# A fourth buffer for loaded weights, and early weights moved behind the last forgetting head, in a two-layer hybrid decoder

## The chip, the cores and the metric

The kernel runs on one core of a Trainium2 chip. The metric is device time in microseconds (us) of one execution, lower is better. Engines are named as in the profile: PE (matrix products), DVE, ACT and POOL (elementwise work), SP (issues the loads of weights).

## The reference

Sixteen learned tokens are put ahead of 512 input tokens (T = 528). Two layers of width 1024 follow. Each normalizes, makes one combined input projection, feeds eight forgetting-attention heads (64 wide) and four retention heads (128 wide), projects their joint output, and ends with a gated feed-forward part of 22 tiles of 128 columns:

```python
proj = einsum('bld,dc->blc', rmsnorm(h, attn_norm_g), w_in)
fq, fk, fv, flog, rq, rk, rv, rg = split(proj)
# forgetting head: s = q.k/sqrt(64) + c[t] - c[s], c = cumsum(log f); softmax over s <= t; then p.v
# retention head: o_t = sum_{s<=t} gamma^(t-s) (q_t.k_s) v_s, in chunks of 128
ret_out = silu(rg) * head_groupnorm(ret, ret_gn_g)
h = h + concat([fox_out, ret_out]) @ w_out
ff = silu(hn @ w_gate) * (hn @ w_up)          # hn = rmsnorm(h, ffn_norm_g)
h = h + ff @ w_down
```

After a last norm the 16 learned tokens are dropped. All is float32.

## The kernel before, in words

Activations are kept transposed, 128 features to a tile and all tokens along it. Every float32 operand is split into a high and a low part (names ending in h and l, or hi and lo): ACT makes the high part by a rounding copy (a "cast"), DVE or POOL subtracts it from the original for the low part, and a product is three products on PE: high by high, high by low, low by high.

Weights come as *jobs*. `fetch` (L161) takes a tile of a ring named `raw`, 512 KB each with three buffers, and has SP load the weight into it. `convert` (L176) makes its high part (ACT, L202) and low part (L205; on POOL for the jobs marked so, in eight pieces of 128 columns). A buffer is free for the next load when the last subtraction has read it. A job is converted some steps ahead of its use, while the job before it is multiplied. `dense_steps` (L208) makes one step per contracted tile of 128; its products are at L228.

The order of PE's work is written out by hand: `merge` and `spread` place the steps of the heads into the steps of the projections, and PE works exactly in that order. The order on ACT, DVE, POOL and SP is set when the program is built by a scheduler that goes by its own costs and by priorities. Each engine works through its own queue strictly in order.

A layer goes through these stages. The two groups of four forgetting heads and four retention heads are worked on while the combined projection still runs. The last forgetting pair, `fox[3]`, and the retention heads 2 and 3 run beside the second round of the output projection (`out_proj(l, 1, ...)`, four jobs `op` for the pairs of output tiles m2 = 0 to 3). The weights of m2 = 2 and 3 go into tiles that earlier heads have left (`spent`: qs0, qs1, kx0, kx1 and rqh, rql, rkh, rkl). Of a forgetting head the change touches this: the probabilities are transposed on PE (L446), cast to `pth` by ACT and `ptl` by DVE (L153, L154, `turn`), and multiplied with the values at L613; ACT copies the result to `ol` at L616, DVE adds it at L617. Of a retention head: its result is squared and cast (`sqh`, L796, ACT; `sq`, `sql`, L797 and L798, DVE), summed by PE at L309 against a tile of ones, and the norm follows (L314 on ACT).

The feed-forward part makes tiles f = 0 and 1 (f < PLAIN) by plain products. From f = 2 on a *Unit* computes gate and up together from seven half-size products in three accumulators, the PSUM banks x, y and z; `keep` copies what x holds at three points of its sum (L1008), and at the third adds bank y to it on DVE (L1011). A unit has a `head`, a `middle` and a `tail` of steps, and between the middle and tail of unit f a part of the down projection of the round before is placed (`down`). Rounds of up to four tiles are multiplied with `w_down` while the next round's units run; the last round's sums stand alone at the end of the layer, eight groups of four steps in layer 0 and sixteen in layer 1, where the real tokens are taken in two parts.

Of the kernel before, what the change touches and what calls it, by code (L numbers as in the profile page):

```python
# [10 lines left out]
F32 = mybir.dt.float32  # L11
# [28 lines left out]
def hybrid_kernel(ctx, tc, x_t, w_in, w_fl, w_out, w_gate, w_up, w_down, vecs, b_fg, rope, decay, mask, ident, out_t):  # L40
# [120 lines left out]
    def fetch(j):  # L161
        job = jobs[j]
        if "load" in job:
            job["load"]()
        elif "raw" not in job:
            n = job["src"].shape[1]
            job["raw"] = wp.tile([128, NK, 128], F32, name="raw", tag="raw", bufs=3)
            if j > 1:
                nc.sync.dma_start(job["raw"], job["src"]) if n == NK else \
                    nc.sync.dma_start(job["raw"][:, 0:n], job["src"])  # L170
# [5 lines left out]
    def convert(j, upto=NK, pinned=False):  # L176

        if j >= len(jobs):
            return
        job = jobs[j]  # L180
        fetch(j)
        if "make" in job:
            if "w" not in job:
                n = job["n"]
                hi, lo = (wring(job["ring"] + p) for p in ("whi", "wlo"))
                job["w"] = [(NK, hi, lo)]
                job["make"](hi[:, 0:n], lo[:, 0:n])
            return
        n = job["src"].shape[1]
        if "w" not in job:  # L190
            job["w"] = job["own"]() if job["own"] else \
                [(NK, *[wring(i) for i in ("whi", "wlo")])]
            job["split"] = 0
        sub = nc.gpsimd.tensor_sub if job["pool"] else nc.vector.tensor_sub
        while job["split"] < min(n, upto):
            c0 = job["split"]
            c1 = min(n, c0 + (2 if j < 2 and c0 < 4 else 4))
            size, hi, lo = job["w"][c0 // job["w"][0][0]]
            o = c0 % size
            hi, lo = hi[:, o:o + c1 - c0], lo[:, o:o + c1 - c0]  # L200
            with tc.high_priority() if j == 5 else ExitStack():
                pin(nc.scalar.copy(hi, job["raw"][:, c0:c1]), pinned)  # L202
            step = 1 if job["pool"] else c1 - c0
            for c in range(0, c1 - c0, step):
                pin(sub(lo[:, c:c + step], job["raw"][:, c0 + c:c0 + c + step], hi[:, c:c + step].bitcast(F32)), pinned)  # L205
            job["split"] = c1

    def dense_steps(src, parts, pool=False, banks=False, ahead=(1, 4), own=None, wait=None, far=False):  # L208

        j = len(jobs)
        jobs.append({"src": src, "pool": pool, "own": own})
# [297 lines left out]
    def fox_steps(g, st, ly, real):  # L511
# [86 lines left out]
        def product(s):  # L598
# [14 lines left out]
                    nc.tensor.matmul(po[:, c0:SEQ], v[:, j, :], pp[:, j, META + c0:T],  # L613
                                     start=(j == 0 and i == 0), stop=(j == 4))
            with tc.high_priority():
                nc.scalar.copy(ol[a0:a1, META:T], po[b0:b1, :])  # L616
                nc.vector.tensor_add(mt[a0:a1, META:T], po[a0:a1, :], ol[a0:a1, META:T])  # L617
            if s == 1:

# [217 lines left out]
                    nc.vector.tensor_add(sv(h[m], real), pv(ps, real), sv(h[m], real))  # L837
        return go

    def out_proj(l, rnd, mix, real):  # L840

        cols = REAL if real else FULL
        xs = lambda k: mix[k]["mix"]
# [1 line left out]
        def spent(m2):  # L845
# [2 lines left out]

        return sum([dense_steps(w_out[l, rnd, m2], [(4 * s, xs, 4, cols, add_h(2 * m2 + s, real)) for s in range(2)],
                                rnd == 0 or m2 < 3, rnd == 1 and m2 == 1, () if rnd == 1 and m2 == 3 else (1, 4),  # L850
                                spent(m2) if rnd == 1 and m2 > 1 else None, far=rnd == 1 and m2 == 1) for m2 in range(NK // 2)], [])

    def ffn(l, st, real, last):
        QC = REAL if real else FULL
# [93 lines left out]
        class Unit:  # L948
# [11 lines left out]

            def load(self):
                if "a" not in self.t:
                    for n, src, pool, tag, bufs in (("a", w_gate, wp, "raw", 3), ("b", w_up, phase["ffn"], "fraw", 2)):
# [39 lines left out]
            def keep(self, i):  # L1003
                def go():
                    if i == 0:
                        self.t["e"] = fft("e", F32, (128, 3, w), 2)
                    with tc.high_priority():
                        nc.scalar.copy(self.t["e"][:, i], self.t["x"][:, 0:w])  # L1008
                        if i == 2:
                            e3 = self.t["e"][:, 2]  # L1010
                            nc.vector.tensor_add(e3, self.t["y"][:, 0:w], e3)  # L1011
                return go

            def done(self):
# [32 lines left out]
        def down_job(p, f0, f1):  # L1047
# [4 lines left out]
            def load():  # L1052
                if t:
                    return
                t["r"] = wp.tile([128, NK, 128], F32, name="raw", tag="raw", bufs=3)
# [38 lines left out]
        for r, (f0, f1) in enumerate(ROUNDS):  # L1094
            for f in range(f0, f1):
# [10 lines left out]
                u = units[f]  # L1106
                u.rest()
                steps += u.middle()
                if f == NF - 1:
                    u.last()  # L1110
                    steps += u.tail()
                p, g0, g1 = fills.pop(0)
                j = down_job(p, g0, g1)
                steps += down(j, 0, 2 * p, g0, g1, not real or f < PLAIN + 2)
                if f < NF - 1:
                    u.last()
                    steps += u.tail()
                steps += down(j, 1, 2 * p + 1, g0, g1, f == PLAIN)
            fills = [(p, f0, f1) for p in range(NK // 2)]
        n = f1 - f0  # L1120
        js = [down_job(p, f0, f1) for p, _, _ in fills]
        if not last:
            for p in range(NK // 2):
                for s in range(2):
                    steps += down(js[p], s, 2 * p + s, f0, f1, False)
        else:


# [13 lines left out]
            for c0, c1 in (PA, PB):  # L1142
                for m in range(NK):
                    ps = []

                    def bank(ps=ps):
                        if not ps:
                            ps.append(psum_a())
                        return ps[0]

                    rnd += product(js[m // 2], m % 2 * n, lambda k, c0=c0, c1=c1: [t[:, c0:c1] for t in acts[f0 + k]],
                                   bank, True, True, n, add_part(m, c0, c1, bank))
# [129 lines left out]
    def layer(l):  # L1282
# [194 lines left out]
```

## Time and profile before

| what | value |
|---|---|
| median of three runs | 1274.67 us (1273.5 to 1275.17) |
| profiled execution | 1274.18 us |
| its span in the trace | 1272.4 us |
| PE busy | 1253.2 us, 98% of the span |
| mean granted clock of PE | 0.992 |
| DVE, ACT, POOL busy | 991.0, 709.1, 296.0 us |

The span is what the trace covers; the profiled execution's own time is 1.8 us longer. A wait in the profile is idle time of an engine, put down to whatever came last. The granted clock is a share of PE's full speed, so 0.50 means that matmuls take twice as long.

### The profile page before, as it was taken

Reading aid. Unit: us, or ns where it says so; the run is one execution under the profiler, and the core shown is the slowest. Engines: PE = TensorE matmul, PEld = TensorE weight load, DVE = VectorE, ACT = ScalarE, POOL = GpSimd, SP = SyncE. Lnnn points to the kernel's source line nnn. Section 1 sums busy time; section 2 is a strip of 40 time slices with the busy share of each in tenths; the row PEclk is TensorE's granted clock in tenths of the full one; section 3 lists DMA queues with packets and bytes.
Section 4 is the critical chain, followed back from the end, with each engine's and each line's share of the span. In section 5 each row is a group of like instructions: output and inputs, shape, how many; then the busy total and the mean of one; then the engine's idle time right before and its main releaser. Section 6 shows DMA issues by size and latency. Waiting matters only on the chain.

```text
span 1272.4 us, 23678 instructions
## 1 busy us (share of the span) xinstructions
PE 1253.2 (98%) x9291; PEld 1199.6 (94%) x9291; DVE 991.0 (78%) x1797; ACT 709.1 (56%) x1313; POOL 296.0 (23%) x584
## 2 busy tenths in 40 slices
PE   9999999899999999999999999998999999999997
PEld 9999999899999999999999988997789999999997
DVE  7887756789987777777776876467899878888875
ACT  7767656676444444444466665566765444444444
POOL 4545655520000000000035555555200000000000
PEclk9999999999999999999999999998999999999999
DMA  6222222221333333332312222222313333333321
GB/s 217 67 76 75 68 69 91 67 100 60 111 113 100 100 100 100 100 100 67 117 60 83 76 75 79 72 76 83 112 59 130 99 100 100 100 101 108 108 67 67
DMA packets 43343, 116.21 MB, mean 91 GB/s; under 512 B 5088, under 2 KB 9952, under 8 KB 43232
## 3 DMA queue, kind: packets, MB, share of 16 engines
q1 hardware_dynamic: 42800, 114.41, 28.1%
q8 instruction: 73, 1.20, 0.4%
q10 hardware_dynamic: 432, 0.29, 0.1%
q14 instruction: 38, 0.31, 0.1%
HBM read 112.58 MB, written 2.10 MB: 90 GB/s over the span
## 4 chain that ended last, share of the span: by engine, by line
PE 94%; DVE 3%; ACT 1%; POOL 1%; DMA 1%; issue 0%; DVEq 0%; ACTq 0%
PE psd L228 28%; PE psa L941 20%; PE psd L941 14%; PE psd L1077 13%; PE psa L228 5%; PE psa L1077 5%; PE psa L613 2%; PE psa L446 2%; PE psa L543 1%; PE psa L783 1%; PE psa L747 1%; POOL wlo L205 1%; PE psa L407 1%; DMA raw<-w_out 1%; PE psa L309 0%
## 5 line engine op out<-in xcount | busy, mean ns | idle before, releaser
L205 POOL TENSOR_TENSOR wlo<-raw,whi 128x128 fp32r<-128x128 f32 x504 | 261.7, 553 | 218.9 <-ACT whi L202 218.8
L228 PE MATMUL psd<-xh,whi 128*128 128x264 f32 (+1 forms) x696 | 170.6, 314 | 0.0
L228 PE MATMUL psd<-xh,wlo 128*128 128x264 f32 (+1 forms) x696 | 161.6, 302 | 0.0
L228 PE MATMUL psd<-xl,whi 128*128 128x264 f32 (+1 forms) x696 | 161.6, 301 | 0.0
L929 ACT CAST fwhi<-raw 128x1024 fp32r<-128x1024 f32 (+1 forms) x64 | 57.7, 902 | 106.8 <-PE psa L941 67.1
L228 PEld LDWEIGHTS psd<-xh,whi 128*128 128x128 f32 x696 | 113.5, 191 | 3.2
L228 PEld LDWEIGHTS psd<-xh,wlo 128*128 128x128 f32 x696 | 111.8, 189 | 4.5
L228 PEld LDWEIGHTS psd<-xl,whi 128*128 128x128 f32 x696 | 112.4, 190 | 2.6
L202 ACT CAST whi<-raw 128x512 fp32r<-128x512 f32 (+1 forms) x140 | 82.3, 612 | 37.7 <-PE psd L228 17.4
L930 DVE TENSOR_TENSOR fwlo<-raw,fwhi 128x1024 fp32r<-128x1024 f32 (+1 forms) x64 | 66.3, 1036 | 29.8 <-ACT fwhi L929 29.8
L125 POOL MEMSET kc<- 64x528 f32 x4 | 2.1, 534 | 371.2 <-PE psd L1077 371.0
L929 ACT CAST whi<-raw 128x1024 fp32r<-128x1024 f32 (+1 forms) x64 | 56.1, 877 | 42.2 <-PE psd L941 40.1
L941 PE MATMUL psa<-th,fwhi 128*128 128x264 f32 (+1 forms) x248 | 70.6, 285 | 0.9 <-ACT e L1008 0.9
L941 PE MATMUL psa<-tl,fwhi 128*128 128x264 f32 (+1 forms) x248 | 70.2, 283 | 0.0
L941 PE MATMUL psa<-th,fwlo 128*128 128x264 f32 (+1 forms) x248 | 70.1, 283 | 0.0
L930 DVE TENSOR_TENSOR wlo<-raw,whi 128x1024 fp32r<-128x1024 f32 (+1 forms) x64 | 64.1, 1002 | 2.1 <-ACT whi L929 2.1
L941 PE MATMUL psa<-th,whi 128*128 128x264 f32 (+1 forms) x232 | 65.5, 282 | 0.0
L941 PE MATMUL psa<-th,wlo 128*128 128x264 f32 (+1 forms) x232 | 65.4, 282 | 0.0
L941 PE MATMUL psa<-tl,whi 128*128 128x264 f32 (+1 forms) x232 | 65.4, 282 | 0.0
L1008 ACT COPY e<-psa 128x264 f32<-128x264 f32 (+1 forms) x120 | 45.0, 375 | 35.7 <-PE psa L941 34.5
L560 ACT ACTIVATE pr<-pr,nmax 128x144 f32<-128x144 f32 (+1 forms) x64 | 36.8, 575 | 45.4 <-DVE nmax L547 26.0
L929 ACT CAST whi<-S 128x1024 fp32r<-128x1024 f32 x22 | 23.1, 1049 | 66.9 <-PE psa L941 65.2
(409 smaller groups left out, 4213.7 us busy)
## 6 DMA issues: line engine op xcount, KB each, us to landing
raw<-w_in SPq DMA_DIRECT2D x54, 512.0 KB, 3.5
raw<-w_gate SPq DMA_DIRECT2D x44, 512.0 KB, 3.9
fraw<-w_up SPq DMA_DIRECT2D x40, 512.0 KB, 3.5
raw<-w_down SPq DMA_DIRECT2D x80, 256.0 KB, 2.9
raw<-w_out SPq DMA_DIRECT2D x16, 512.0 KB, 3.4
h<-x_t SPq DMA_DIRECT2D x8, 264.0 KB, 4.5
dec<-decay SPq DMA_DIRECT2D x8, 264.0 KB, 2.7
raw<-w_up SPq DMA_DIRECT2D x4, 512.0 KB, 3.4
```

What stands on the lines that cost most here:

```text
L202: pin(nc.scalar.copy(hi, job["raw"][:, c0:c1]), pinned)
L205: pin(sub(lo[:, c:c + step], job["raw"][:, c0 + c:c0 + c + step], hi[:, c:c + step].bitcast(F32)), pinned)
L228: nc.tensor.matmul(ps[1][b][:, 0:c1 - c0], w[:, wk, :], x[:, c0:c1], start=(k == 0 and i == 0), stop=(k == n - 1 and i == 2))
L407: nc.tensor.matmul(ps[:, 0:c1 - c0], wf[k // HB][:, k % HB, :], st["x"][k][part][:, c0:c1], start=(i == 0), stop=(i == 2 * NK - 1))
L446: nc.tensor.transpose(ps[:, 128 * j:128 * j + 128], src[:, o:o + 128], idt)
L560: nc.scalar.activation(pr, pr, AF.Exp, bias=nmax[0:nq], scale=-1.0, accum_out=rsum)
L613: nc.tensor.matmul(po[:, c0:SEQ], v[:, j, :], pp[:, j, META + c0:T], start=(j == 0 and i == 0), stop=(j == 4))
L929: nc.scalar.copy(hi, src)
L930: nc.vector.tensor_sub(lo, src, hi.bitcast(F32))
L941: nc.tensor.matmul(bank()[:, 0:b.shape[-1]], a[:, o + k, :], b, start=(fresh and k == 0 and i == 0), stop=(k == n - 1 and i == 2), skip_gr ...
L1008: nc.scalar.copy(self.t["e"][:, i], self.t["x"][:, 0:w])
L1077: nc.tensor.matmul(v[:, 0:c1 - c0], a[:, s * n + k, :], b[:, c0:c1], start=(k == 0 and i == 0), stop=(k == n - 1 and i == 2))
```

## The change

1. The ring `raw` has four buffers in place of three, for all jobs.
2. The casts of the output projection's weights m2 = 2 and 3 (round 1) may be placed on ACT only after the copy at L616 of the last forgetting head.
3. For f = 2 and 3 ACT copies the bank y into the tile `sq`, and DVE's addition in `keep` reads that tile.
4. In the last unit (f = 21) the first of the two down projections stands between middle and tail, as in all other units.
5. The last round's sums are woven: of the first two groups (layer 0) or three (layer 1) the first three steps come first, then the fourth step of each.

```diff
-            job["raw"] = wp.tile([128, NK, 128], F32, name="raw", tag="raw", bufs=3)
+            job["raw"] = wp.tile([128, NK, 128], F32, name="raw", tag="raw", bufs=4)
...
-            with tc.high_priority() if j == 5 else ExitStack():
+            with tc.high_priority() if j == 5 else tc.issue_after(job["after"]()) if job["after"] else ExitStack():
                 pin(nc.scalar.copy(hi, job["raw"][:, c0:c1]), pinned)
...
             with tc.high_priority():
-                nc.scalar.copy(ol[a0:a1, META:T], po[b0:b1, :])
+                st["last"] = nc.scalar.copy(ol[a0:a1, META:T], po[b0:b1, :]).ins
...
-                                spent(m2) if rnd == 1 and m2 > 1 else None, far=rnd == 1 and m2 == 1) for m2 in range(NK // 2)], [])
+                                spent(m2) if rnd == 1 and m2 > 1 else None, far=rnd == 1 and m2 == 1, after=after if m2 > 1 else None) for m2 in range(NK // 2)], [])
...
-                            nc.vector.tensor_add(e3, self.t["y"][:, 0:w], e3)
+                            y = self.t["y"][:, 0:w]
+                            if self.f < PLAIN + 2:
+                                y = tt("sq")[:, 0:w]
+                                nc.scalar.copy(y, self.t["y"][:, 0:w])
+                            nc.vector.tensor_add(e3, y, e3)
...
                 u.rest()
                 steps += u.middle()
-                if f == NF - 1:
-                    u.last()
-                    steps += u.tail()
                 p, g0, g1 = fills.pop(0)
                 j = down_job(p, g0, g1)
                 steps += down(j, 0, 2 * p, g0, g1, not real or f < PLAIN + 2)
-                if f < NF - 1:
-                    u.last()
-                    steps += u.tail()
+                u.last()
+                steps += u.tail()
                 steps += down(j, 1, 2 * p + 1, g0, g1, f == PLAIN)
...
+        def woven(groups, n0):
+            g = groups[:n0]
+            return [f for p in g for f in p[:-1]] + [p[-1] for p in g] + [f for p in groups[n0:] for f in p]
+
         if not last:
-            for p in range(NK // 2):
-                for s in range(2):
-                    steps += down(js[p], s, 2 * p + s, f0, f1, False)
+            steps += woven([down(js[p], s, 2 * p + s, f0, f1, False) for p in range(NK // 2) for s in range(2)], 2)
...
+            rnd = woven(rnd, 3)
...
-        op = out_proj(l, 1, mixes[1], real)
+        op = out_proj(l, 1, mixes[1], real, lambda: fox[3]["last"])
```

How the instructions move on ACT, where layer 0's last forgetting head has its probabilities cast (psa to pth). qs0 and kx0 are weights of m2 = 2, whi is a weight of m2 = 0. Before:

```order
L153 CAST pth_122<-psa_3618 128x2x128
L202 CAST qs0_3937<-raw_3935 128x512
L153 CAST pth_122<-psa_3661 128x3x128
L153 CAST rvh_3629<-sq_3639 128x512
L715 CAST rvh_3629<-sq_3644 64x128
L716 CAST rvl_3630<-sq_3644 64x128
L202 CAST kx0_3939<-raw_3935 128x512
L153 CAST pth_122<-psa_3679 128x4x128
L202 CAST whi_3763<-raw_3761 128x512
```

With the change:

```order
L153 CAST pth_122<-psa_3618 128x2x128
L153 CAST pth_122<-psa_3661 128x3x128
L153 CAST rvh_3629<-sq_3639 128x512
L715 CAST rvh_3629<-sq_3644 64x128
L716 CAST rvl_3630<-sq_3644 64x128
L153 CAST pth_122<-psa_3679 128x4x128
L202 CAST whi_3763<-raw_3761 128x512
```

The two weight casts are gone from between the casts of probabilities and values.

ACT again, some 15 instructions later, up to the norm of retention head 2, whose square is sqh (fwhi is the first gate weight; rqh and rkh are weights of m2 = 3). Before:

```order
L153 CAST mxh2_3743<-mixt_2953 128x528
L789 COPY d_3775<-psa_3779 128x16
L202 CAST rqh_3948<-raw_3946 128x512
L202 CAST rkh_3950<-raw_3946 128x512
L202 CAST fwhi_3993<-raw_3991 128x512
L791 COPY d_3775<-psa_3774 128x512
L202 CAST fwhi_3993<-raw_3991 128x512
L796 ACTIVATE sqh_3808<-d_3775 128x528
L314 ACTIVATE r_3842<-psa_3836,epsc_91 128x264
```

With the change:

```order
L153 CAST mxh2_3743<-mixt_2953 128x528
L789 COPY d_3775<-psa_3779 128x16
L202 CAST whi_3763<-raw_3761 128x512
L202 CAST qs0_3937<-raw_3935 128x512
L202 CAST rqh_3948<-raw_3946 128x512
L202 CAST kx0_3939<-raw_3935 128x512
L791 COPY d_3775<-psa_3774 128x512
L202 CAST rkh_3950<-raw_3946 128x512
L796 ACTIVATE sqh_3808<-d_3775 128x528
L202 CAST fwhi_3993<-raw_3991 128x512
L314 ACTIVATE r_3842<-psa_3836,epsc_91 128x264
```

Between mxh2 and sqh stood four casts of weights beside the copies L789 and L791; now there are five, and the casts of the gate weight stand behind sqh.

PE at the first sums of layer 0's last round (ah5 and al5 are the last unit's activation, psd one accumulator per group). Before:

```order
L1077 MATMUL psd_8203<-ah4_7977,wlo_8107 128x264 x2
L1077 MATMUL psd_8203<-ah5_8131,whi_8106 128x264 x2
L1077 MATMUL psd_8203<-al5_8132,whi_8106 128x264 x2
L1077 MATMUL psd_8203<-ah5_8131,wlo_8107 128x264 x2
L1077 MATMUL psd_8229<-ah2_7599,whi_8106 128x264 x2
```

With the change:

```order
L1081 MATMUL psd_8226<-ah4_7981,wlo_8099 128x264 x2
L1081 MATMUL psd_8207<-ah5_8170,whi_8098 128x264 x2
L1081 MATMUL psd_8207<-al5_8171,whi_8098 128x264 x2
L1081 MATMUL psd_8207<-ah5_8170,wlo_8099 128x264 x2
L1081 MATMUL psd_8226<-ah5_8170,whi_8098 128x264 x2
```

The first group's last step now stands behind the first three steps of the second group as well.

More of the change, by code (lines that the diff above doesn't have):

```diff
@@ L206, in convert, with dense_steps @@
             job["split"] = c1
-    def dense_steps(src, parts, pool=False, banks=False, ahead=(1, 4), own=None, wait=None, far=False):
+    def dense_steps(src, parts, pool=False, banks=False, ahead=(1, 4), own=None, wait=None, far=False, after=None):
         j = len(jobs)
-        jobs.append({"src": src, "pool": pool, "own": own})
+        jobs.append({"src": src, "pool": pool, "own": own, "after": after})
         def chunk(k0, k, n, xs, cols, ps, done):
@@ L838, in add_h, with out_proj @@
         return go
-    def out_proj(l, rnd, mix, real):
+    def out_proj(l, rnd, mix, real, after=None):
         cols = REAL if real else FULL
@@ L962, in load @@
                 if "a" not in self.t:
-                    for n, src, pool, tag, bufs in (("a", w_gate, wp, "raw", 3), ("b", w_up, phase["ffn"], "fraw", 2)):
+                    for n, src, pool, tag, bufs in (("a", w_gate, wp, "raw", 4), ("b", w_up, phase["ffn"], "fraw", 2)):
                         self.t[n] = pool.tile([128, NK, 128], F32, name=tag, tag=tag, bufs=bufs)
@@ L1054, in load @@
                     return
-                t["r"] = wp.tile([128, NK, 128], F32, name="raw", tag="raw", bufs=3)
+                t["r"] = wp.tile([128, NK, 128], F32, name="raw", tag="raw", bufs=4)
                 for s in range(2):
@@ L1149, in bank @@
                         return ps[0]
-                    rnd += product(js[m // 2], m % 2 * n, lambda k, c0=c0, c1=c1: [t[:, c0:c1] for t in acts[f0 + k]],
-                                   bank, True, True, n, add_part(m, c0, c1, bank))
+                    rnd.append(product(js[m // 2], m % 2 * n, lambda k, c0=c0, c1=c1: [t[:, c0:c1] for t in acts[f0 + k]],
+                                   bank, True, True, n, add_part(m, c0, c1, bank)))
+            rnd = woven(rnd, 3)
             def scale_a(m):
```

## The prediction

> **What bounds the kernel now.** I read, in this order: the page's first part, the waits of TensorE, the timeline at the two longest of them, and the busy time and granted clock in stretches around them.
>
> ```profile
> PE 1253.2 (98%) x9291; PEld 1199.6 (94%) x9291; DVE 991.0 (78%) x1797; ACT 709.1 (56%) x1313; POOL 296.0 (23%) x584
> ```
>
> TensorE (PE) is busy for 98% of the span, and the change keeps its matmuls. So an edit is worth only what it takes from PE's idle time or gives back in clock. The longest of PE's waits inside the layers (total us, times, longest us):
>
> ```profile
> PE psa L613 <- ACT pth L153: 6.2, 2, 3.2
> PE psd L941 <- DVE e L1011: 1.1, 1, 1.1
> PE psa L941 <- ACT e L1008: 0.9, 2, 0.5
> ```
>
> The 6.2 us is one stall per layer at L613, the product of a forgetting head. The timeline (start, duration, engine, line, in brackets the idle time before and its end) shows the one in layer 0:
>
> ```profile
> 244.17 0.87 DVE L711 SCALAR_TENSOR_TENSOR sq<-mean,psa 128x512 f32<-128x512 f32 x2
> 246.88 0.62 ACT L202 CAST qs<-raw 128x512 fp32r<-128x512 f32 x1 [5.16 <-DMA raw<-w_out]
> 247.78 0.62 ACT L153 CAST rvh<-sq 128x512 fp32r<-128x512 f32 x1
> 248.93 0.62 ACT L202 CAST kx<-raw 128x512 fp32r<-128x512 f32 x1
> 249.45 0.58 ACT L153 CAST pth<-psa 128x512 fp32r<-128x512 f32 x1
> 250.06 0.69 DVE L154 TENSOR_TENSOR ptl<-psa,pth 128x512 fp32r<-128x512 f32 x1 [0.19 <-ACT pth L153]
> 250.08 0.79 PE L613 MATMUL psa<-pth,vv 128*128 128x512 f32 x1 [3.19 <-ACT pth L153]
> 250.81 0.79 PE L613 MATMUL psa<-ptl,vv 128*128 128x512 f32 x1
> ```
>
> ACT works its queue in order. It stands 5.16 us before the cast of an output-projection weight (qs) whose load has not landed. The cast of the transposed probabilities (pth), which PE needs at L613, stands behind qs, the casts of rvh and rvl, and kx. Layer 1 has the same picture:
>
> ```profile
> 878.07 0.62 ACT L202 CAST qs<-raw 128x512 fp32r<-128x512 f32 x1 [4.62 <-DMA raw<-w_out]
> 881.26 0.80 PE L613 MATMUL psa<-pth,vv 128*128 128x512 f32 x1 [3.04 <-ACT pth L153]
> 882.24 0.79 PE L613 MATMUL psa<-ptl,vv 128*128 128x512 f32 x1 [0.18 <-DVE ptl L154]
> ```
>
> The stretches add something that the waits do not count (columns: stretch, its length, busy us of PE, PE's loads, DVE, ACT, POOL, then granted clock, DMA share, GB/s):
>
> ```profile
> 246.90:250.00 3.10, 0.00 (x0) 0.00 (x0) 1.93 (x3) 3.06 (x8) 2.42 (x5) 0.91 0.00 0
> 253.50:256.20 2.70, 2.70 (x14) 2.70 (x14) 1.32 (x2) 2.65 (x4) 1.61 (x4) 0.50 0.34 118
> 256.40:259.80 3.40, 3.40 (x26) 3.27 (x25) 3.09 (x6) 3.13 (x7) 0.00 (x0) 1.00 0.41 146
> 1266.70:1272.00 5.30, 0.00 (x0) 0.00 (x0) 2.04 (x4) 0.00 (x0) 0.00 (x0) 0.50 0.67 224
> ```
>
> The clock falls in the idle stretch: a mean of 0.91 over 3.10 us is full speed up to about 249.44 and half from there. It is 0.50 up to some 256.25, between the second row and the third, although PE never idles in the second, and then 1.00 again: 6.8 us at half speed. PE's work from the second L613 at 250.81 to 256.25 thus took 5.44 us and needs half of that. A stall here costs its idle time and then 2.72 us of slow clock.
>
> **The change, part by part.** *Buffers and the moved casts (layer 0).* The load of qs was issued only when a buffer of the ring came free, as POOL ended its subtractions:
>
> ```profile
> 229.29 4.88 POOL L205 TENSOR_TENSOR wlo<-raw,whi 128x128 fp32r<-128x128 f32 x8 [4.36 <-ACT whi L202]
> 239.23 4.20 POOL L205 TENSOR_TENSOR wlo<-raw,whi 128x128 fp32r<-128x128 f32 x8 [5.06 <-ACT whi L202]
> raw<-w_out SPq DMA_DIRECT2D x16, 512.0 KB, 3.4
> ```
>
> With a fourth buffer the qs/kx weight takes the one freed at 234.17, and the rqh/rkh weight the one freed at 243.43. At 3.4 us per load (the last row) both land by 246.9. The casts themselves now come after the copy at L616 in ACT's queue, so nothing of them stands before pth. ACT's critical start is then sq (DVE, done at 245.04). The rvh and rvl casts take 248.93 − 247.78 = 1.15 to the next start, so pth runs 246.19 to 246.77, ptl starts at 246.80, and the second L613 follows 0.75 later as before: 247.55 instead of 250.81, 3.26 earlier. Some 0.4 of the wait stays; it is too short to halve the clock, if the wait of 1.1 at L941 is a guide, after which the clock did not drop. The 5.44 us at half clock become 2.72. PE arrives at the head norm's first L309 **5.98** earlier.
>
> There the moved casts are met again. The rows of that place:
>
> ```profile
> 251.35 0.54 ACT L757 CAST rsh<-sd 128x416 fp32r<-128x416 f32 x1 [0.61 <-DVE sd L752]
> 257.28 0.63 ACT L153 CAST mxh<-mixt 128x528 fp32r<-128x528 f32 x1
> 258.40 0.62 ACT L202 CAST rkh<-raw 128x512 fp32r<-128x512 f32 x1
> 258.92 0.62 ACT L202 CAST fwhi<-raw 128x512 fp32r<-128x512 f32 x1
> 261.40 0.65 ACT L796 ACTIVATE sqh<-d 128x528 fp32r<-128x528 f32 x1
> 262.24 0.70 DVE L798 TENSOR_TENSOR sql<-sq,sqh 128x528 fp32r<-128x528 f32 x1
> 262.47 0.40 PE L309 MATMUL psa<-sqh,ones 128*128 128x264 f32 x2
> 263.00 0.51 PE L309 MATMUL psa<-sql,ones 128*128 128x264 f32 x2
> 265.36 0.95 DVE L321 TENSOR_TENSOR nwt<-r 128x528 f32<-128x528 f32 x1 [0.38 <-ACT r L320]
> ```
>
> PE comes at 262.47 − 5.98 = 256.49. ACT has its own chain: rsh starts 1.29 after ptl (251.35 − 250.06), at 248.09. From there to the cast mxh of mixt are 5.93 of steady ACT work (257.28 − 251.35), of which one weight cast (0.62) is moved behind: 253.40. Then, by the new order, come whi, qs, rqh, kx, the copy L791 and rkh, six steps of 0.52 (258.92 − 258.40) after mxh's 0.60: sqh runs 257.12 to 257.77. PE waits **1.28**. DVE has rkl ahead of sql. Each takes 0.70 to 0.95, the upper figure being what the L321 row of the same width took; POOL now subtracts at the same time, so I take the upper one: sql ends at 259.0. PE's first two L309 (0.40) end at 258.2, so it waits a second time, about 0.9. The second pair starts at 259.05 instead of 263.00: **−3.95**. Bounds: −5.98 if ACT and DVE keep up, and −0.55 if these waits halve the clock for 6.8 us once more (3.4 lost).
>
> *The same in layer 1.*
>
> ```profile
> 893.35 0.40 PE L309 MATMUL psa<-sqh,ones 128*128 128x512 f32 x1
> 893.94 0.50 PE L309 MATMUL psa<-sql,ones 128*128 128x512 f32 x1 [0.20 <-DVE sql L798]
> ```
>
> PE's work before L613 ends at 881.26 − 3.04 = 878.22, so the second L613 goes from 882.24 to about 878.45, 3.8 earlier; and I take layer 0's 2.72 for the slow clock. PE is at L309 some 6.5 earlier, at 886.85. Only whi, qs, rqh, L791 and kx come before sqh there, one weight cast and a 16-column copy fewer: by the same steps sqh ends at 888.04 (wait 1.2), sql at about 888.8, and rkl stands behind it. 893.94 becomes 888.8: **−5.1**. Bounds: −6.5 and −1.7 (by the same two reasons).
>
> *The bank copied (f=2).* PE waits 1.1 at L941 since the addition of a PSUM bank sits behind two 1.2 us subtractions of DVE:
>
> ```profile
> 322.46 0.37 ACT L1008 COPY e<-psa 128x264 f32<-128x264 f32 x1
> 325.23 0.43 DVE L1011 TENSOR_TENSOR e<-psd,e 128x264 f32<-128x264 f32 x1
> 950.97 0.36 ACT L1008 COPY e<-psa 128x256 f32<-128x256 f32 x1
> ```
>
> Now ACT copies the bank (some 0.37, as the row of the same shape) and PE is released then, at about 322.85. The copy of bank x comes 0.37 later, and PE wants that bank at 323.02, so some 0.2 is lost again: **−0.9**. In layer 1 no wait stands at this place, but the x copy ends at 951.33 and PE takes the bank at once, so the inserted copy delays it: **+0.3** (0 to 0.4). f=3 has no wait in either layer and I take nothing.
>
> *The last unit and the woven sums.* PE's 0.9 at L1008 are two waits of 0.5 before the tail of unit 21, where nothing lies between middle and tail. A down projection now stands there, 24 (layer 1: 12) matmuls over 2 us: both waits go. What is late next is al, the low half of the last activation:
>
> ```profile
> 617.56 0.41 PE L1077 MATMUL psa<-ah,fwhi 128*128 128x264 f32 x2
> 624.23 0.70 DVE L154 TENSOR_TENSOR al<-tq,ah 128x528 fp32r<-128x528 f32 x1
> 1233.61 0.41 PE L1077 MATMUL psd<-ah,fwhi 128*128 128x512 f32 x1
> 1239.94 0.68 DVE L154 TENSOR_TENSOR al<-tq,ah 128x512 fp32r<-128x512 f32 x1
> ```
>
> It came 7.37 and 7.01 after the tail. One down projection less covers it (2.8 us), but the woven groups bring 9 matmuls of another group (or two) ahead of the chunk that needs it: some 7.3 us in layer 0, 6.2 in layer 1, and in both DVE has one add and one subtraction fewer inside that chain. **−0.46** and **−0.3** (bounds 0 and −0.5 each, if the chain does not shrink).
>
> Sum: −3.95 − 5.1 − 0.9 + 0.3 − 0.46 − 0.3 = −10.4. Against the profiled execution's 1274.18 that is 1263.8. The median of the runs, 1274.67, lies 0.5 above that execution: **1264**.
>
> The Trainium skill, "TensorE: Matmul & The Clock Gate", section "Why this matters for your kernels", says that gaps in TensorE's work of more than about 3 us bring the half clock, and its Part 1 puts that down to one idle, free-running window of about 3.4 us. By that rule the two short waits at L309 would leave the clock alone, which is the forecast's side. The trace agrees only in part: idle stretches of 3.19 and 3.04 us, shorter than the window, did bring it, so the window need not be wholly idle.
>
> *SP's queue.* The loads move with the buffers: the first gate weight now takes the buffer of the projection weight whose last cast (whi) ACT makes at about 254, so it is issued when POOL has subtracted it, and lands perhaps 3.4 later, near 260. In layer 0 one of its casts stands ahead of ACT's L314, the next step of the head norm after L309. That norm's result is used by the last chunks of the projection only, and I price it at nothing; if it were late by 1 us, PE would lose at most that.
>
> **The rivals.** *B, no wait at L309.* ACT's and DVE's chains keep up, because PE's slow clock fed some of the steps that I took as steady. For it: every ACT step is also fed by PE. Against: rsh to mxh has two table loads and leaves no idle time. It adds 2.03 + 1.4: 1260.6.
>
> *C, the clock falls at L309.* Idle 1.28 + 0.9 with 0.40 busy between is 2.2 idle in a stretch of 2.6. The clock fell within the 3.1 us row above, and in the row after 1266.70 it was low from the start, 2.2 us after the last matmul; the 1.1 us wait brought no drop. So 2.2 is between, and I cannot tell which side it falls on. An episode as long as at L613, 6.8 at half clock, loses 3.4 where PE has work throughout. One layer: 1267.7; both: 1271.1.
>
> *D, the wait only moves.* PE waits at L309 in each layer as long as it did at L613 (3.2 and 3.0) with the half clock: the head casts are worth nothing, and 1264 + 9.05 = 1273 to 1274. It would need sqh about 2 us later than worked out.
>
> *E, slower.* The moved casts meet their loads late again, now with the head norm's sqh behind them in ACT's queue, and the wait of 5.16 and 4.62 comes on top of 1.28 and 1.2, with the clock's 3.4 twice: 9.8 + 6.8 − 10.4 = 6.2 slower, 1281. It decides from a wait of 3 us per layer at L309, where the gain is spent. Against it: the buffers are freed at 234.17 and 243.43, and the casts come at about 254, 7 us after the landing.
>
> That the fourth buffer does nothing by itself can be too: had the qs load kept its place it would still land at 246.9, ahead of its cast at about 254. The time would be A's.
>
> **How the numbers follow.** Forecast A 0.42, B 0.16, C 0.32, D 0.06, E 0.04. A's own range is 1262 to 1266, from the sql step (0.7 or 0.95, both layers), the ±0.5 of the small edits and the runs' spread. The range for 8 in 10 is 1259.5 to 1271.5: B to both drops of C. About 0.2% (2.5 us) is what a measurement can tell from no change; A, B and C lie beyond it: faster 0.90, D same 0.06, E slower 0.04.
>
> **What would show it.** Right: no stall over 0.6 at L613 in PE's waits, no load wait before qs on ACT, clock 1.00 in the stretches after L613, new waits of PE at L309 on sqh and sql of about 1 us each, none at L1011 and none at L1008 for the last unit. C shows as a granted clock of 0.50 just after L309. B shows as no L309 rows in the waits. Wrong would be a wait on a load of w_out, w_gate or w_up ahead of L796 or L314 on ACT, or al before the last sums with over 0.5 us.

## The result and the profile after

The changed kernel takes 1267.95 us (median of six runs, 1266.39 to 1268.77) against 1274.45 for the kernel before (six runs, 1273.11 to 1275.5): a ratio of 0.9949, 95% interval 0.9936 to 0.9961. It is faster by some 6.5 us; 10.4 were forecast. The profiled execution took 1266.39, the fastest of the six, with a span of 1264.6. Traces are compared with that of before (1274.18), and differ by 7.8.

One name of the section on the change has to be put right: the head norm with sqh (L796) is that of retention head 3, the last one.

The longest of PE's waits inside the layers, in the changed kernel (total us, times, longest us):

```profile
PE psa L309 <- DVE sql L798: 1.6, 2, 0.9
PE psa L309 <- ACT sqh L796: 1.6, 2, 0.8
...
PE psa L941 <- DVE al L154: 0.9, 1, 0.9
PE psd L228 <- DVE h L837: 0.8, 1, 0.8
...
PE psa L941 <- ACT e L1008: 0.2, 1, 0.2
```

The 6.2 us at L613 and the 1.1 at L941 for the bank are gone. Two waits at L309 per layer have come in, as forecast, and two at places that the forecast priced at nothing or nearly so: one for an addition at L837, one for al.

The place in layer 0 where the moved casts now stand (timeline: start, duration, engine, line, idle time before):

```profile
246.05 0.59 ACT L153 CAST pth<-psa 128x512 fp32r<-128x512 f32 x1
...
247.41 0.50 PE L613 MATMUL psa<-ptl,vv 128*128 128x512 f32 x1
...
253.24 0.63 ACT L153 CAST mxh<-mixt 128x528 fp32r<-128x528 f32 x1
...
256.40 0.62 ACT L202 CAST rkh<-raw 128x512 fp32r<-128x512 f32 x1
256.92 0.65 ACT L796 ACTIVATE sqh<-d 128x528 fp32r<-128x528 f32 x1
...
257.62 0.51 PE L309 MATMUL psa<-sqh,ones 128*128 128x264 f32 x2 [0.82 <-ACT sqh L796]
258.07 0.95 DVE L798 TENSOR_TENSOR sql<-sq,sqh 128x528 fp32r<-128x528 f32 x1
259.08 0.52 PE L309 MATMUL psa<-sql,ones 128*128 128x264 f32 x2 [0.95 <-DVE sql L798]
```

These were worked out as 246.19, 247.55, 253.40, 257.12 for sqh and 259.05 for the second L309: none is off by more than 0.2. PE comes to the first L309 0.3 later than worked out, so its first wait is 0.82 and not 1.28. What comes right behind is seen in the stretches (length, busy us of PE, PE's loads, DVE, ACT, POOL, granted clock, DMA share, GB/s):

```profile
256.40:259.80 3.40, 1.63 (x12) 1.20 (x11) 2.49 (x4) 1.17 (x3) 3.40 (x6) 1.00 0.51 154
259.90:263.20 3.30, 3.30 (x17) 3.30 (x16) 2.06 (x3) 3.08 (x6) 3.12 (x7) 0.50 0.11 24
```

After the two waits the clock is 0.50 for one stretch, as in rival C, though for 3.4 us and not 6.8. In layer 1 the waits are 0.77 and 0.66 and no slow clock follows. There the new wait stands some 20 us later:

```profile
883.47 3.06 POOL L205 TENSOR_TENSOR qs<-raw,qs 128x128 fp32r<-128x128 f32 x4
886.49 2.22 POOL L205 TENSOR_TENSOR kx<-raw,kx 128x128 fp32r<-128x128 f32 x4
888.67 6.18 POOL L205 TENSOR_TENSOR wlo<-raw,whi 128x128 fp32r<-128x128 f32 x8
...
894.88 0.33 SPq L169 DMA_DIRECT2D raw<-w_up  x1
...
898.47 0.62 ACT L202 CAST whi<-raw 128x512 fp32r<-128x512 f32 x1 [3.27 <-DMA raw<-w_up]
...
902.85 0.68 DVE L837 TENSOR_TENSOR h<-psd,h 128x512 f32<-128x512 f32 x1
903.59 0.50 PE L228 MATMUL psd<-mxh,rqh 128*128 128x512 f32 x1 [0.75 <-DVE h L837]
```

Read from below: PE wants an accumulator that DVE has to empty (L837). Ahead of that addition DVE's queue has the subtraction for the second up weight (f = 1), whose cast waits 3.27 on ACT for its load. SP issues that load at 894.88, when POOL has made the last piece of an earlier weight (888.67 + 6.18 = 894.85) and so freed the buffer. POOL came to that weight late, because it now makes the low parts of qs and kx at 883 to 889. (That this is not the whole cause is seen below, where DVE makes them.) Before, POOL made them at 879 to 883, for the most part while PE stood at L613 (878.22 to 881.26):

```profile
878.76 1.69 POOL L205 TENSOR_TENSOR qs<-raw,qs 128x128 fp32r<-128x128 f32 x4 [4.09 <-ACT qs L202]
880.41 2.19 POOL L205 TENSOR_TENSOR kx<-raw,kx 128x128 fp32r<-128x128 f32 x4
```

Set side by side (us), with each difference read at the same instruction in both traces:

| place | forecast | traces |
|---|---|---|
| layer 0, up to the second L309 | −3.95 | −3.92 |
| clock after L309, layer 0 | 0 | +1.52 |
| bank of f = 2, layer 0 | −0.9 | −1.22 |
| last unit and woven sums, layer 0 | −0.46 | −0.36 |
| layer 1, up to the second L309 | −5.1 | −4.98 |
| L837, layer 1 | 0 | +0.94 |
| bank of f = 2, layer 1 | +0.3 | +0.31 |
| last unit and woven sums, layer 1 | −0.3 | −0.06 |
| sum | −10.4 | −7.77 |

### The profile page after: what moved, and what is told of

Read it like the earlier page. It is cut to its first block, busy times and chain, and to the rows that moved or that the text cites. A ratio compares the mean times of both kernels' runs of the same rounds, so it can differ in the third digit from the quotient of the medians.

```text
span 1264.6 us, 23684 instructions
## 1 busy us (share of the span) xinstructions
PE 1249.0 (99%) x9291; PEld 1196.1 (95%) x9291; DVE 991.8 (78%) x1797; ACT 709.8 (56%) x1317; POOL 302.2 (24%) x584
## 5 line engine op out<-in xcount | busy, mean ns | idle before, releaser
L941 PE MATMUL psa<-th,fwhi 128*128 128x264 f32 (+1 forms) x248 | 70.6, 284 | 0.3 <-ACT e L1008 0.2
L941 PE MATMUL psa<-tl,fwhi 128*128 128x264 f32 (+1 forms) x248 | 70.2, 283 | 0.0
L941 PE MATMUL psa<-th,fwlo 128*128 128x264 f32 (+1 forms) x248 | 70.2, 283 | 0.0
L941 PE MATMUL psa<-th,whi 128*128 128x264 f32 (+1 forms) x232 | 65.6, 283 | 0.0
L941 PE MATMUL psa<-th,wlo 128*128 128x264 f32 (+1 forms) x232 | 65.5, 282 | 0.0
L941 PE MATMUL psa<-tl,whi 128*128 128x264 f32 (+1 forms) x232 | 65.4, 282 | 0.0
L1008 ACT COPY e<-psa 128x264 f32<-128x264 f32 (+1 forms) x120 | 45.0, 375 | 36.3 <-PE psa L941 35.1
```

Source lines behind the costliest of these rows:

```text
L941: nc.tensor.matmul(bank()[:, 0:b.shape[-1]], a[:, o + k, :], b, start=(fresh and k == 0 and i == 0), stop=(k == n - 1 and i == 2), skip_gr ...
```

## The experiments

Times are medians; the kernel before ran on the same chip in each of three groups (1274.49, 1274.85 and 1274.17).

**Parts alone.** The first group takes the change apart. The heads' parts alone (fourth buffer and moved casts; nothing else of the diff):

> The fourth buffer and the moved casts alone, without the copied bank, the reordered last unit and the woven sums. Reading of the two traces: the heads' part is worth -3.9 in layer 0 before a half-clock stretch takes 1.5 of it back, and -4.9 in layer 1 before a late addition (L837) takes 0.95 back: some -6.4 us against the kernel before, where the whole change has -6.5 by medians. Rival: the small edits cost as much as they bring or the clock takes more, and this kernel is as fast as the whole change or faster (-7 or more).

Measured: 1267.64, ratio 0.9947 (0.9935 to 0.996), −6.85. So the heads' parts carry the gain, and the rest adds nothing that the runs can tell. The trace shows the same two waits at L309 in both layers, yet the clock stays up. These are its stretches at the place of layer 0 shown above:

```profile
256.40:259.80 3.40, 1.61 (x12) 1.19 (x10) 3.12 (x4) 1.80 (x4) 3.40 (x5) 1.00 0.37 112
259.90:263.20 3.30, 3.30 (x28) 3.30 (x28) 1.36 (x2) 2.40 (x5) 3.06 (x8) 1.00 0.09 37
```

PE is as idle as in the changed kernel (1.61 busy, 1.63 there) and is granted 1.00 behind it, not 0.50. Instead PE waits 0.72 us for L837 in layer 0 as well, as it does in layer 1. Where the clock falls, PE comes later to that place, and the addition is no longer late: layer 0 pays one of the two.

The fourth buffer alone:

```diff
-            job["raw"] = wp.tile([128, NK, 128], F32, name="raw", tag="raw", bufs=3)
+            job["raw"] = wp.tile([128, NK, 128], F32, name="raw", tag="raw", bufs=4)
```

(and the same at the two other places of the ring)

> The fourth buffer alone. Theory P (the place of a cast in ACT's queue decides): qs and kx now land early and are cast early, so the stall at L613 goes, but the first gate weight's cast is now placed ahead of the head norm's sqh (L796), while its buffer comes free only when POOL has subtracted the first output-projection weight: ACT then stands some 5 us for that load, PE waits 4 to 6 us at L309 in each layer with the half clock, and the kernel is between 2 us faster and 5 us slower than before. Theory L (the late load is all that was wrong): the stall goes and nothing takes its place, -9 to -12 us.

Measured: 1272.89, ratio 0.9989 (0.9981 to 0.9998), −1.6. The range was met, the mechanism only in part. The stalls at L613 are gone, but the scheduler now puts the qs cast ahead of other heads' work, where its load is again late:

```profile
869.66 0.62 ACT L202 CAST qs<-raw 128x512 fp32r<-128x512 f32 x1 [2.79 <-DMA raw<-w_out]
```

```profile
PE psa L309 <- DVE sql L798: 3.4, 2, 2.0
PE psa L446 <- DVE pd L668: 2.1, 1, 2.1
PE psa L309 <- ACT sqh L796: 1.6, 2, 0.9
...
PE psa L228 <- ACT whi L202: 1.3, 1, 1.3
PE psd L228 <- DVE sg L674: 1.1, 1, 1.1
```

The first fence is ACT in layer 1, the second lists PE's waits. The 2.1 us at L446 follow from that cast: pd is late on DVE behind a part that waited for ACT. The stall of 5 us before sqh on the gate weight's load, which I expected, is not there. Theory L falls all the same: landing the load early is worth little while the cast's place is free to move.

The moved casts alone, with three buffers (the diff's lines with `after`, without the ring):

> The moved casts alone, with three buffers. The qs weight lands at the same time as before, but its casts stand behind the copy at L616; the rqh and rkh weight lands after the head norm, and only three weight casts are left ahead of sqh. Theory P: no stall at L613, at L309 a wait of under 0.8 us in all per layer and no half clock: -10 to -12 us, faster than the whole change; the fourth buffer is what lets two more casts in ahead of sqh. Theory L: the weights of the last two jobs land too late without the fourth buffer, and PE waits for them in the projection or the first gate tiles by several us; no more than -5 us.

Measured: 1268.29, ratio 0.9953 (0.994 to 0.9967), −6.2. Both theories had part of it. L309 has only 0.4 and 1.2 us of waits, as theory P said, and no slow clock. But the weights land later, and PE waits for additions that stand behind them in DVE's queue:

```profile
PE psd L228 <- DVE h L837: 3.6, 3, 2.4
```

So the moved casts are as fast as with the fourth buffer (1267.64): what is saved at L309 is lost at L837.

The small edits alone (bank, last unit, woven sums):

> The copied bank, the reordered last unit and the woven sums alone, with three buffers and the casts where they were. By the two traces: -1.1 for the bank in layer 0, +0.2 to +0.3 in layer 1, -0.4 for the last unit in layer 0 and about 0 in layer 1, where a wait for al of 0.86 takes the place of the one removed: -1.2 us in all. Rival, the forecast's terms: -1.4 us with no wait for al. A third: the stalls at L613 stay and nothing else is seen, within 0.5 us of the kernel before.

Measured: 1273.79, ratio 0.9998 (0.9989 to 1.0006): no difference that can be told. Its waits show why:

```profile
PE psa L613 <- ACT pth L153: 6.3, 2, 3.3
...
PE psa L941 <- DVE al L154: 0.9, 1, 0.9
PE psa L941 <- ACT e L1008: 0.8, 1, 0.8
```

The bank's wait of 1.1 is gone, and 5 us later PE waits 0.8 at L1008 for the next unit's copy, which was on time before. The waits ahead of the tail are gone, and in layer 1 al is late by 0.9.

**What took the rest.** The second group repeats the change, and moves its casts and POOL's pieces.

> The changed kernel once more, for one question: whether the half-clock stretch after layer 0's L309 belongs to the kernel. If two waits of about 0.8 and 0.9 with 0.4 busy between them always bring it, a second profile shows it again at that place. If it hangs on where the stretch falls against the clock's own steps, this profile may show it in layer 0, in layer 1 or in neither (the heads alone had the same waits and no slow clock); where it is missing in layer 0, PE instead waits some 0.7 us for L837 there, as it does in layer 1.

Measured: 1267.56, ratio 0.9942 (0.9928 to 0.9955). The clock fell in layer 0 again, at the same distance from the place where it first rose. On this, more below.

The casts of m2 = 2 and 3 behind sqh:

```diff
-                            nc.scalar.activation(sv(sh, real), sv(d, real), AF.Square)
+                            behind[l] = nc.scalar.activation(sv(sh, real), sv(d, real), AF.Square).ins
...
-        op = out_proj(l, 1, mixes[1], real, lambda: fox[3]["last"])
+        op = out_proj(l, 1, mixes[1], real, lambda: behind[l])
```

> The changed kernel with one thing moved on: the casts of m2 = 2 and 3 stand behind the head norm's sqh (L796) in place of the copy at L616. Theory Q (only the queueing at L309 is lost): its waits of 1.6 to 1.8 us per layer go and the time falls by about 3 us against the change, to 1264.5. Theory R (behind it POOL sets the pace: it subtracts qs, kx and the next weights one after the other, frees the buffer for w_up, and DVE's L837 follows that load): the waits at L309 go, but PE waits as much longer at L837, and the time is within 1 us of the change.

Measured: 1269.25, ratio 0.9956 (0.9943 to 0.9968), 1.7 above the change in the same group (the ranges do not overlap). PE's longest waits:

```profile
PE psd L229 <- DVE h L838: 3.9, 2, 2.1
PE psa L229 <- POOL wlo L206: 1.9, 3, 1.0
```

(The lines are one further on in this kernel.) The waits at L309 are gone, and 5.8 us stand at the addition and at POOL itself in place of the 3.2 at L309 and the 0.8 at L837: the mechanism is theory R's, and its time is not: it expected less than 1 us either way. In the profiled execution the clock falls too, behind the wait at L838 in layer 1.

The low parts of qs and kx on DVE, with the casts where the change has them:

```diff
-                                rnd == 0 or m2 < 3, rnd == 1 and m2 == 1, () if rnd == 1 and m2 == 3 else (1, 4),
+                                rnd == 0 or m2 < 2, rnd == 1 and m2 == 1, () if rnd == 1 and m2 == 3 else (1, 4),
```

> The changed kernel with the low parts of m2 = 2 (qs, kx) made by DVE in two pieces in place of POOL in eight. POOL is then free some 5 us sooner. Theory R: w_up lands 2 to 5 us sooner and the wait at L837 goes in both layers (-0.7 to -0.95 each), while L309 gets worse, since DVE has two more subtractions of 0.7 to 0.9 ahead of sql: some +0.5 to +1.5 per layer; in sum from -1 to +2 us against the change. If the wait at L837 stays, POOL is not what paces it.

Measured: 1268.38, ratio 0.9949 (0.9937 to 0.9962), 0.8 above the change; the ranges overlap. The total is within what was expected; the wait at L837 is not:

```profile
PE psa L309 <- DVE sql L798: 2.9, 2, 1.5
PE psa L309 <- ACT sqh L796: 1.6, 2, 0.8
...
PE psd L228 <- DVE sg L674: 1.1, 1, 1.1
...
PE psd L228 <- DVE h L837: 0.8, 1, 0.8
```

L309 became worse, as DVE has two more subtractions ahead of sql, and L837 still costs 0.8 in layer 1. POOL is idle for 5.3 us there before the projection weight that frees w_up's buffer. That weight's cast (whi) stood on ACT behind a gate weight whose load was 3.7 us late. So POOL alone does not set the pace: what counts is when the buffer is freed, and ACT's order and POOL's work both go into that.

Both together:

> Both: the casts behind sqh, and the low parts of m2 = 2 on DVE. Theory R: no wait over 0.5 us at L309 or at L837, no half clock; -1.6 to -1.8 per layer at L309 and -0.95 at L837 per layer (in layer 0 instead the 1.5 of slow clock): 4 to 5 us faster than the change, 1263 to 1264. Theory Q: the same as the casts behind sqh alone. If another wait takes their place (the norm's L314 behind three casts, or rkl late), it shows at the projection's last weights, and the gain is smaller.

Measured: 1262.61 (1262.26 to 1262.93), ratio 0.9903 (0.9889 to 0.9916): 12.2 us faster than before, and 5.0 faster than the change in the same group. Of PE's waits two are left beyond those of the first 60 us, which all these kernels have:

```profile
PE psa L942 <- DVE al L154: 0.9, 1, 0.9
PE psa L942 <- ACT e L1009: 0.8, 1, 0.8
```

None is left at L309 or at the addition, and the clock does not fall until the end. One of the two moves made the time worse, the other did so or nothing, and both together bring 5 us. Each alone only hands the time to another queue. How much of the late load is POOL's and how much ACT's was not taken apart further.

**The last unit, the buffer and the bank again.** In the changed kernel, layer 1 (the first row is PE's first matmul behind the tail):

```profile
1227.88 0.40 PE L1081 MATMUL psd<-ah,whi 128*128 128x512 f32 x1
...
1232.22 1.05 ACT L929 CAST whi<-raw 128x1024 fp32r<-128x1024 f32 x1
1233.17 0.62 ACT L153 CAST ah<-tq 128x512 fp32r<-128x512 f32 x1
...
1233.30 1.23 DVE L930 TENSOR_TENSOR wlo<-raw,whi 128x1024 fp32r<-128x1024 f32 x1 [0.40 <-ACT whi L929]
1234.44 0.68 DVE L154 TENSOR_TENSOR al<-tq,ah 128x512 fp32r<-128x512 f32 x1
...
1235.18 0.39 PE L941 MATMUL psa<-al,whi 128*128 128x272 f32 x1 [0.86 <-DVE al L154]
```

A down weight's cast and its subtraction stand ahead of ah and al. An edit places them behind, in the last round of each layer (`held` is set for p = 2, and `st["act"]` holds the two instructions that make ah and al):

```diff
+            def make(hi, lo):
+                with tc.issue_after(st["act"][0]) if held else ExitStack():
+                    with tc.issue_after(st["act"][1]) if held else ExitStack():
+                        splits(hi, lo, t["r"][:, 0:2 * n])
```

> The changed kernel with one weight moved: in the last round of each layer the third down weight (p = 2) is split only after the last unit's activation (ah, al). In layer 1 its cast (1.05) and its subtraction (1.23) now stand ahead of ah and al and PE waits 0.86 us for al. Theory: that wait goes, al comes some 0.9 us sooner, and the time falls by 0.5 to 0.9 us, which the runs may just tell; PE then needs that weight some 3 us after al, so nothing new is late. Rival (the chain of al is paced by its own steps, silu and the additions): the wait stays within 0.2 us and the time is the same.

Measured on the change: 1266.57, ratio 0.9941 (0.9929 to 0.9953). No wait for al is left in the trace, and there PE gains 0.9 against the changed kernel (the difference at the same instruction of both traces, ahead of that place and at it). The medians cannot show it: the change was measured in two other groups, and against the kernel before of its own group this one gains 7.6, where the change gained 6.5 and 7.3. The profiled execution (1268.45) is the slowest of the five; it is 2.0 us behind the changed kernel's within the first 40 us already.

All three moves together:

> The casts behind sqh, the low parts of m2 = 2 on DVE, and the third down weight behind the last activation. By addition, 1262.6 - 0.9: 1261.5 to 1262.5, some 12 to 13 us faster than the kernel before, no half clock in any layer, and as the longest wait that of 0.85 at L1008 (f = 3 in layer 0). If the terms do not add, the time is that of the two without the last (1262.6) or slower.

Measured: 1260.42 (1259.73 to 1260.59), ratio 0.9889 (0.9874 to 0.9905), 13.8 us faster than before and better than forecast by 1, of which some 0.7 is the group: the kernel before, too, is 0.7 faster in it. It is the fastest version: the casts behind sqh, qs and kx on DVE, the down weight behind al. All that is left of its waits after the first 60 us:

```profile
PE psd L229 <- DVE h L838: 0.4, 1, 0.4
PE psa L942 <- ACT e L1009: 0.3, 1, 0.3
```

Against the two moves alone it gains 2.2 in the traces, of which the wait for al is 0.9 and that at L1009 0.5; 0.4 is lost at L838. About 1 us arises in the first 40 us, which the edit does not touch; where PE starts within them differs by up to 2 us from one profile to the next, and I have not found out why. So the third move is worth 0.9 at its place; the rest is not shown to be its work.

The same with three buffers:

> The same as the kernel with all three, with three buffers in place of four. Theory (the loads of w_out and w_gate follow the release of buffers, and now nothing else is late): rqh and rkh land only after the first output-projection weight is subtracted (about 259.7), the first gate and up weights later still, and PE waits 2 to 4 us per layer at L837 or at the first gate tile, as the moved casts alone did (2.4 us in layer 0): 2 to 6 us slower than with four. Rival (the fourth buffer has no part once the casts are moved): within 0.8 us of it.

Measured: 1262.83 (1262.67 to 1263.47), ratio 0.9911 (0.9897 to 0.9924), 2.4 above the same kernel with four buffers. The waits at the addition are back with 2.1 us (1.6 the longest), and 0.7 stands at L942. So the fourth buffer is worth 2.4 us once nothing else holds up the same places. Beside the moved casts alone it was worth nothing that can be told (1267.64 against 1268.29), and by itself 1.6.

The same without the copied bank:

> The same as the kernel with all three, without the copied bank (f = 2 and 3 add from the bank, as before). Theory T (the next wait takes it): the 1.1 us wait at L941 for the addition comes back, and the wait of 0.6 to 0.85 at L1008 of the next unit, which DVE paces, goes down by as much: the time is within 0.5 us. Rival, the forecast's term: 0.6 us slower (0.9 in layer 0, less 0.3 in layer 1).

Measured: 1260.98 (1260.32 to 1262.64), ratio 0.9897 (0.9884 to 0.9911), 0.6 above the kernel with the bank copied; the ranges overlap. Theory T expected the 1.1 us wait back, and it is not in the list of waits:

```profile
PE psd L229 <- DVE h L838: 2.1, 1, 2.1
...
PE psa L942 <- ACT e L1009: 0.6, 1, 0.6
```

In this profile the addition is 2.1 late after a load that came some 2 us later than in the kernel above, and this execution (1262.64) is the slowest of the four. With PE 2 us later, the addition from the bank is in time. What the copied bank is worth in the fast version stays open; it is under 1 us.

## Why the prediction was right and wrong

**Right.** The stall at L613, its cause and its price in the profiled execution: idle 3.2 and 3.0 and some 2.7 of slow clock, all of it gone. The new queue at L309 and its time, layer by layer, to 0.2 us. That the loads would land in time (rival E): no cast of m2 = 2 and 3 waits for its load. The measured time lies within the stated range, but outside A's own (1262 to 1266). It is 0.25 above C's 1267.7 for one layer, the second likeliest, and that nearness is in part luck: C put 3.4 on the clock, which cost 1.5 in the trace; the 0.9 at L837 and the 1.3 by which traces and medians differ made up the rest.

Two of the signs of being wrong came. The wait for al is 0.86 in layer 1, over the 0.5 named. And in layer 0 ACT waits for the load of the first gate weight ahead of L314:

```profile
260.10 0.62 ACT L202 CAST fwhi<-raw 128x512 fp32r<-128x512 f32 x1 [2.53 <-DMA raw<-w_gate]
```

That load landed near 260, as worked out, and PE has no wait in the head norm behind it: at this place the price of nothing held.

**Wrong, first step: "I price it at nothing".** This is the paragraph on SP's queue. It followed the first gate weight's buffer only. The forecast counted the moved casts on ACT and rkl on DVE, but not the eight subtractions on POOL that make the low parts of qs and kx (5.3 us of work). While PE stood at L613, these cost PE nothing. Moved behind it, they fall in a stretch where POOL works without a gap (881.27 to 899.12 in layer 1) and delay the freeing of buffers, the loads of the gate and up weights, and the additions at L837. It cost 0.9 us in layer 1, and in layer 0 either that or the clock. I also looked for the late load only at L314, in the head norm, and not at the DVE queue behind the weights. The two moves together, and neither alone, show what was lost: 5.0 us lie at L309, its clock, and this chain.

**Wrong, second: the clock.** Forecast A put nothing on the clock behind two waits of about 1 us. That they can bring it down was rival C, at 0.32. The clock fell in layer 0 in both profiles of the changed kernel, for +1.5 us, and in neither layer of the heads alone.

**Wrong, third: "one add and one subtraction fewer" ahead of al.** I put 0.3 us on layer 1 and got 0.1. The chain from the tail's end at 1227.88 to al at 1235.12 is 7.2 us, not shorter than the 7.0 before: one addition left it, but both subtractions of down weights (1.23 each) stayed, the second now right ahead of al.

**Sized right, worth less.** The copied bank gave its 1.1 us at the place. With the small edits alone 0.8 of it was taken back at the next unit's copy.

## What to carry to other kernels

When work is moved out of a stall, list every engine on which it runs, and ask what each of them was doing at the new place; a stall hides work on all engines, not only on the one that is blamed. A place in an in-order queue is worth more than an early load: a cast whose load is in time still blocks whatever stands behind it. Where two queues feed the same wait, edit both before judging either: here one alone made the time 1.7 us longer, the other 0.8 or nothing, and both made it 5.0 shorter.

## What the runs showed of the clock

The two waits at L309 brought the half clock in some kernels and not in others, with the same idle time. It becomes plain when time is cut into steps of 3.413 us (the length of the changed kernel's slow stretch; those of the kernel before last two of them, 6.827), counted from the instant at which the clock first rose in each execution. All changes of the clock in all 14 profiles lie on such steps (71 and 256 steps later in the kernel before, 74 in the changed one), the last fall behind the end of the matmuls too. Summing PE's idle time in each step at full clock, worked out from the matmuls' starts and ends:

```
idle in one step of 3.413 us        clock in the next step
2.67  2.54  (kernel before)         0.5   0.5
2.57  1.74  (small edits alone)     0.5   0.5
2.31  (low parts on DVE)            0.5
2.12  (fourth buffer alone)         0.5
1.83  (casts behind sqh)            0.5
1.79  1.77  (the change, twice)     0.5   0.5
1.63  (no bank copy, last run)      1.0
1.53  (moved casts alone)           1.0
1.49  (casts behind sqh, layer 0)   1.0
1.38  (heads alone, L309, layer 0)  1.0
```

The rows at 1.0 are the longest idle times that stayed without a drop, but for three of 1.42 to 1.49 in the fourth buffer alone and the weight behind al. Every step with 1.74 us idle or more is followed by the half clock, none with 1.63 or less. So in these traces it takes about half a step, in one piece or in several, and a stall of 2.4 us that straddles two steps (the moved casts alone at L837) costs no clock. The Trainium skill, "TensorE: Matmul & The Clock Gate", Part 1, has the step, free-running and 3.413 us long, and asks for an idle one; the step agrees, and these rows say that half an idle one is enough. Steps at half clock with 0.55 to 1.52 us idle were followed by another slow one, steps with none by full speed: a slow stretch lasts one step or two.

This is why the changed kernel's 1.77 idle at L309 cost 1.5 us more in layer 0, and the heads' parts alone, where a step ended within the first of the two waits, paid nothing. It is a matter of where the waits fall, and that I could not read from the trace of the kernel before. The half was read off these traces afterwards, and no run was made to test it.

Nor is the slow clock at L613 a fixed price. The profiled execution of the kernel before has four slow steps and a mean clock of 0.992, and each step takes 0.0013 off the mean. Of its 21 executions in the first group nine have 0.992 (median 1274.73 us) and five 0.996 (median 1273.63), which leaves room for two slow steps at most beside the slow stretch behind the last matmul. The forecast took 2.72 us per layer, from one execution, for all of them; this may be a part of why the traces differ by 7.8 and the medians by 6.5.
